# Three MLPs on one Trainium2 core: 2x2 blocks with seven block products in place of eight

## The chip, the core and the metric

The kernel runs on one core of a Trainium2 chip. Five engines work side by side, each through its own queue and in that queue's order: PE (TensorE, matrix products into PSUM), DVE (VectorE), ACT (ScalarE), POOL (GpSimd) and SP (SyncE), which here issues most of the DMAs. The metric is the device time of one execution in microseconds; the median of three runs is quoted.

## What is computed

Three blocks follow each other on 1024 tokens of 1024 features in float32. Each has a mixer (gated delta rule and neighbourhood attention; sliding-window attention and a convolution; gated linear attention) with an output projection, and an MLP of width 4096 with a residual and norms around it. The change is in the MLPs. Cut to the first:

```python
x = layer_norm(DEEPNORM_ALPHA * x + mix, ln1_g[l], ln1_b[l])
ff = jnp.square(jax.nn.relu(jnp.einsum('btd,df->btf', x, w1[l]) + b1[l]))
ff = jnp.einsum('btf,fd->btd', ff, w2[l]) + b2[l]
x = layer_norm(DEEPNORM_ALPHA * x + ff, ln2_g[l], ln2_b[l])
```

The other two have no bias, a residual without factor, and RMS norms; the second norm of the last block gives the output.

## The kernel before

**Exact products.** A float32 operand is kept as a high part (rounded by an ACT cast) and a low part (the rest, a DVE subtraction). `mm3` (L215 to L219) makes a product from three: high by high, high by low, low by high. `unit` (L198) loads up to 1024 elements per partition of a weight matrix into one of two `raw` tiles and splits them into one of `wbufs` = 4 tiles `whi` and `wlo`.

**Order of the work.** The program is written in one sequence; the library places each engine's instructions in a queue when the kernel is built, by priority, and adds the waits. Weights are moved ahead (`high_priority`, `UP` = 6000 instructions); nothing else in the MLPs is ordered by hand. Row tiles pass their norms in stages (`pipe`, `advance`, `flush`): each call takes every row tile under way one stage further.

**PSUM.** Eight banks: two tiles `d` of two banks (`psd`), two tiles `m` and two tiles `s` of one bank each (`psm`, `psp`; `psy` takes them in turn).

**Around an MLP** (`out_mlp`). First come the output projection's products for each row tile of 128 tokens, their addition to the residual X (8 row tiles in SBUF), and the norm, whose last stage `to_xt` (L325) transposes the row tile (8 transposes on PE) and splits it into XT, feature-major, in two halves of 512 tokens (`xt0`, `xt1`). Then `up(f)` makes 128 hidden features for all tokens: 2 token halves x 8 k x 3 products with N = 512, Relu and square on ACT, the square again on POOL and the low part on DVE (L1077 to L1082). `fm_two` makes the first two such blocks, both for the first half of the tokens before the second half, between which the pending row tiles are finished. After five blocks the loop over c (8 steps) takes four hidden blocks, multiplies them with 512 rows of w2 for each token tile t and column half (4 k x 3 products) and adds the result to X on DVE (L1109), and makes the next four hidden blocks. In the last step each row tile of X is complete after its two halves and `done` norms it for the next block or for the output.

**Places.** The two halves of XT, the mixer's output and the hidden tiles live in pools that alternate between the two sides of SBUF. The hidden layer never leaves SBUF.

## Time and profile before

| | us |
|---|---|
| median of three runs | 3921.47 |
| lowest, highest | 3918.44, 3923.11 |
| span of the profiled execution | 3909.3 |
| PE busy | 3723.6 (95%) |
| DVE busy | 1734.8 (44%) |
| ACT busy | 1131.1 (29%) |
| POOL busy | 744.4 (19%) |

The span runs from the first to the last instruction of the program; the profile gives no other time for that execution, so 12.2 us lie between its span and the median. Matmuls overlap on PE, so their durations don't add up: the distance between the starts of two is what one costs. The first MLP runs from about 817 to 1531, the second from about 1982 to 2705, the third ends the kernel.

### The profile page before, as it was taken

What the parts mean: (1) busy time and instruction counts of PE and PEld (TensorE: products, weight loads), DVE (VectorE), ACT (ScalarE), POOL (GpSimd) and SP (SyncE); (2) the same over time, 40 slices, a digit from 0 to 9 for tenths busy, and PEclk for the clock granted to TensorE, in tenths of its full rate; (3) what the DMA queues carried; (4) which work ended last, traced back from release to release, by engine and by line L of the source; (5) the groups of instructions that cost most, each with busy time, mean ns of one, the idle gap of its engine ahead of it and who ended that gap; (6) DMA issues with size and microseconds to landing.
All of it is one profiled execution on the core that took longest, in us unless ns stands there. A gap on an engine that the chain in (4) does not pass through costs nothing.

```text
span 3909.3 us, 46321 instructions
## 1 busy us (share of the span) xinstructions
PE 3723.6 (95%) x19060; PEld 3045.7 (78%) x19060; DVE 1734.8 (44%) x2844; ACT 1131.1 (29%) x1889; POOL 744.4 (19%) x583
## 2 busy tenths in 40 slices
PE   8898898999999999878999999999999999999999
PEld 7777776678888887666778888888788878888887
DVE  7676625552222327896532222224536342222223
ACT  3233334431111123447531111113422231111112
POOL 2011113231200004677310000001112100000001
PEclk9999999999999999988999999999999999999999
DMA  4212235221111112211111111111111211111111
GB/s 158 66 48 57 71 127 172 70 54 49 49 44 44 49 60 98 49 33 33 60 54 44 44 43 43 56 58 43 43 59 49 92 60 49 49 49 44 44 43 70
DMA packets 247160, 237.14 MB, mean 61 GB/s; under 512 B 39467, under 2 KB 208872, under 8 KB 246308
## 3 DMA queue, kind: packets, MB, share of 16 engines
q1 hardware_dynamic: 243492, 227.88, 19.5%
q10 hardware_dynamic: 3456, 6.29, 0.4%
q8 instruction: 150, 2.46, 0.3%
q14 instruction: 62, 0.51, 0.0%
HBM read 197.96 MB, written 36.18 MB: 60 GB/s over the span
## 4 chain that ended last, share of the span: by engine, by line
PE 50%; DVE 5%; issue 2%; POOL 2%; ACT 1%; DMA 0%; POOLq 0%; DVEq 0%; ACTq 0%
PE d L217 8%; PE d L219 8%; PE d L218 8%; PE s L219 4%; PE m L217 4%; PE s L218 4%; PE s L217 4%; PE m L219 4%; PE m L218 4%; PE s L1849 1%; DVE acc L1259 1%; DVE t L1259 1%; POOL st L1253 1%; DVE wlo L206 1%; PE d L1466 1%
## 5 line engine op out<-in xcount | busy, mean ns | idle before, releaser
L206 ACT CAST whi<-raw 128x1024 fp32r<-128x1024 f32 (+1 forms) x283 | 293.8, 1048 | 1751.8 <-PE d L218 657.4
L206 DVE TENSOR_TENSOR wlo<-raw,whi 128x1024 fp32r<-128x1024 f32 (+1 forms) x283 | 355.1, 1263 | 684.6 <-ACT whi L206 684.1
L1081 POOL TENSOR_TENSOR r<-r 128x1024 f32<-128x1024 f32 x96 | 181.8, 1894 | 1778.3 <-ACT hh L1080 1758.0
L217 PE MATMUL d<-xt0h,whi 128*128 128x512 f32 x1152 | 461.2, 400 | 7.1 <-DVE X L1385 5.8
L219 PE MATMUL d<-xt0h,wlo 128*128 128x512 f32 x1152 | 459.7, 399 | 7.6 <-DVE wlo L206 7.6
L218 PE MATMUL d<-xt0l,whi 128*128 128x512 f32 x1152 | 458.9, 398 | 0.0
L217 PE MATMUL d<-xt1h,whi 128*128 128x512 f32 (+1 forms) x1152 | 449.8, 391 | 0.3
L219 PE MATMUL d<-xt1h,wlo 128*128 128x512 f32 (+1 forms) x1152 | 448.9, 390 | 0.0
L218 PE MATMUL d<-xt1l,whi 128*128 128x512 f32 (+1 forms) x1152 | 448.5, 389 | 0.0
L219 PE MATMUL m<-whi,hl 128*128 128x512 f32 x768 | 303.9, 396 | 1.5 <-DVE hl L1082 1.5
L219 PE MATMUL s<-whi,hl 128*128 128x512 f32 x768 | 303.9, 396 | 0.6 <-DVE hl L1082 0.6
L218 PE MATMUL m<-wlo,hh 128*128 128x512 f32 x768 | 303.1, 395 | 0.0
L218 PE MATMUL s<-wlo,hh 128*128 128x512 f32 x768 | 302.5, 394 | 0.0
L217 PE MATMUL m<-whi,hh 128*128 128x512 f32 x768 | 301.2, 392 | 0.1
L217 PE MATMUL s<-whi,hh 128*128 128x512 f32 x768 | 301.3, 392 | 0.0
L219 PEld LDWEIGHTS d<-xt0h,wlo 128*128 128x128 f32 x1152 | 218.5, 190 | 60.8 <-DVE wlo L206 15.9
L217 PEld LDWEIGHTS d<-xt0h,whi 128*128 128x128 f32 x1152 | 218.9, 190 | 54.9 <-issue 8.3
L1109 DVE TENSOR_TENSOR X<-X,m 128x512 f32<-128x512 f32 x184 | 126.2, 686 | 292.2 <-PE m L219 292.0
L218 PEld LDWEIGHTS d<-xt0l,whi 128*128 128x128 f32 x1152 | 218.8, 190 | 45.7 <-issue 0.9
L218 PEld LDWEIGHTS d<-xt1l,whi 128*128 128x128 f32 x1152 | 218.3, 190 | 44.3 <-DVE xt1l L335 1.5
L217 PEld LDWEIGHTS d<-xt1h,whi 128*128 128x128 f32 x1152 | 217.9, 189 | 43.9 <-ACT xt1h L334 1.2
L219 PEld LDWEIGHTS d<-xt1h,wlo 128*128 128x128 f32 x1152 | 218.5, 190 | 42.8 <-issue 0.2
(523 smaller groups left out, 6485.6 us busy)
## 6 DMA issues: line engine op xcount, KB each, us to landing
raw<-in_w_dram SPq DMA_DIRECT2D x64, 512.0 KB
raw<-in_w_in_dram SPq DMA_DIRECT2D x62, 512.0 KB
raw<-in_w_mlp_up_dram SPq DMA_DIRECT2D x32, 512.0 KB
raw<-in_w_mlp_down_dram SPq DMA_DIRECT2D x32, 512.0 KB
raw<-in_w_up_dram SPq DMA_DIRECT2D x32, 512.0 KB
raw<-in_w_down_dram SPq DMA_DIRECT2D x32, 512.0 KB
raw<-in_w_out_dram SPq DMA_DIRECT2D x24, 512.0 KB
X<-xres SPq DMA_DIRECT2D x12, 512.0 KB
```

Source lines behind the costliest of these rows:

```text
L206: self.split = nc.scalar.copy(hi, raw), nc.vector.tensor_tensor(lo, raw, f32v(hi), op=ALU.subtract), ld
L217: mm(out, ah, bh, start=first, stop=False)
L218: mm(out, ah, bl, start=False, stop=False)
L219: mm(out, al, bh, start=False, stop=last)
L1081: nc.gpsimd.tensor_tensor(r, r, r, op=ALU.mult)
L1109: V.tensor_tensor(xs, xs, p, op=ALU.add)
L1253: P.tensor_tensor(ac[:, q : q + 512], ac[:, q : q + 512], tp, op=ALU.add)
L1259: V.scalar_tensor_tensor(out=ac[:, q : q + wd], in0=h[:, q + k : q + k + wd], scalar=cw[:, n, k : k + 1], in1=ac[:, q : q + wd], op0=ALU.m ...
L1466: T.matmul(pd[:, a + 4 * g], PT[:, g, k], vt[:, t + 1 - nk + k, 64 * g : 64 * g + 64], start=k == 0, stop=k == nk - 1)
L1849: T.matmul(ps[g][:, 128 * c : 128 * c + 128], a, x, start=True, stop=True)
```

## The change

Each MLP product is cut into 2x2 blocks, and seven block products (Winograd's form of Strassen's method) take the place of eight. For the up product the blocks are halves of the tokens and halves of the features on one side, and halves of the features and pairs of 128 hidden columns on the other.

- `feed` takes the place of `to_xt` in the norms before an MLP: it keeps the transposed row tile as it is (`a1`, `a2`), splits the blocks that are used alone (L[0], L[1], L[6]) and, from the second half of the tokens on, makes sums on POOL and DVE. `feed_sums` then splits the four sums (L[2] to L[5]).
- The row tiles of X go to DRAM (`spill`) and are added back in the down pass.
- `up_pair` makes 2 x 128 hidden columns for all tokens: `up_weights` loads and combines the weights, seven products of 12 matmuls each go into three banks (`p_`, `r_`, `q_`), ACT and DVE take partial results out while later products add to the same banks, and the four hidden blocks with three of their sums are written to DRAM (`hd`), from one of two places in X.
- After all 16 pairs the down pass runs 4 steps c of 7 products s: for each s the layer's block is loaded from `hd` and split (ACT, POOL), the weights' block is split (ACT, DVE), with sums on POOL at s = 2, and 4 token tiles x 12 matmuls follow. Results are added into quarters of X: s = 5 of the last step completes the first four row tiles, s = 6 the other four.
- The pools of the two XT halves and the mixer's output become fixed places p0 to p3 that stay, with three more (q0 to q2) in the MLPs; block 3's mixer pool changes sides, and block 2 keeps five transposed query tiles instead of six.

The core of the diff (the removed `out_mlp` is printed above):

```diff
+    def mm3(self, out, ah, al, bh, bl, first, last, more=False):
...
+    def slot(self, tag, shape, dt=F32R):
+        pool = self.qp if tag[0] == "q" else self.pa if tag < "p2" else self.pb
+        return self.t(pool, shape, dt, tag=tag)
...
+    def feed(self, t, y):
+        nc = self.nc
+        V, A, T, P = nc.vector, nc.scalar, nc.tensor, nc.gpsimd
+        L = self.L
+        if t == 0:
+            L.update({n: self.slot(f"q{n}", [128, 2, 4, 512]) for n in (0, 1)})
+            L["a1"] = self.slot("q2", [128, 2, 4, 512], F32)
+        if t == 4:
+            L["a2"] = self.slot("p0", [128, 2, 4, 512], F32)
+            L[6] = self.slot("p1", [128, 2, 4, 512])
+        ts = slice(128 * (t % 4), 128 * (t % 4) + 128)
+        raw = L["a1" if t < 4 else "a2"]
+        for q in range(2):
+            p = self.psm().rearrange("p (k c) -> p k c", k=4)
+            for k in range(4):
+                T.transpose(p[:, k], y[:, (4 * q + k) * 128 : (4 * q + k + 1) * 128], self.ident)
+            A.copy(raw[:, q, :, ts], p)
+            if t < 4 or q:
+                o = L[q if t < 4 else 6]
+                A.copy(o[:, 0, :, ts], p)
+                V.tensor_tensor(o[:, 1, :, ts], p, f32v(o[:, 0, :, ts]), op=ALU.subtract)
+        if t >= 4:
+            a1 = L["a1"]
+            s1, s3 = (x[:, :, ts] for x in self.sums())
+            P.tensor_tensor(s1, raw[:, 0, :, ts], raw[:, 1, :, ts], op=ALU.add)
+            V.tensor_tensor(s3, a1[:, 0, :, ts], raw[:, 0, :, ts], op=ALU.subtract)
+            P.tensor_tensor(a1[:, 0, :, ts], s1, a1[:, 0, :, ts], op=ALU.subtract)
+    def sums(self):
+        return [self.X[:, 2 * n : 2 * n + 2].rearrange("p t (k c) -> p (t k) c", k=2) for n in range(2)]
+    def halves(self, o, x):
+        for k in (slice(0, 2), slice(2, 4)):
+            self.nc.scalar.copy(o[:, 0, k], x[:, k])
+            self.nc.vector.tensor_tensor(o[:, 1, k], x[:, k], f32v(o[:, 0, k]), op=ALU.subtract)
+    def feed_sums(self):
+        L = self.L
+        a1 = L["a1"]
+        s1, s3 = self.sums()
+        L[2] = self.slot("p0", [128, 2, 4, 512])
+        self.halves(L[2], a1[:, 0])
+        L[3] = self.slot("p2", [128, 2, 4, 512])
+        self.halves(L[3], s1)
+        L[4] = self.slot("p3", [128, 2, 4, 512])
+        self.halves(L[4], s3)
+        self.nc.vector.tensor_tensor(s1, a1[:, 1], a1[:, 0], op=ALU.subtract)
+        L[5] = self.slot("q2", [128, 2, 4, 512])
+        self.halves(L[5], s1)
+    def parts(self, x, n):
+        nc = self.nc
+        hi, lo = (self.t(self.wp, [128, self.WN], F32R, tag=tag, bufs=self.wbufs)[:, :n] for tag in ("whi", "wlo"))
+        if len(x.shape) == 3:
+            hi, lo = (y.rearrange("p (a b) -> p a b", a=x.shape[1]) for y in (hi, lo))
+        nc.scalar.copy(hi, x)
+        nc.vector.tensor_tensor(lo, x, f32v(hi), op=ALU.subtract)
+        return hi, lo
+    def up_weights(self, w1v, p):
+        nc = self.nc
+        V = nc.vector
+        with self.tc.high_priority(offset=UP):
+            raw = []
+            for q in range(2):
+                r = self.t(self.wp, [128, self.WN], tag="raw", bufs=2).rearrange("p (a b) -> p a b", a=8)
+                nc.sync.dma_start(out=r, in_=w1v[:, :, 256 * p + 128 * q : 256 * p + 128 * q + 128])
+                raw.append(r)
+            b1, b2 = raw
+            u = self.parts(b1, 1024)
+            ta = self.t4().rearrange("p (a b) -> p a b", a=8)
+            V.tensor_tensor(ta[:, 4:], b2[:, :4], b1[:, :4], op=ALU.subtract)
+            V.tensor_tensor(ta[:, :4], b2[:, 4:], ta[:, 4:], op=ALU.subtract)
+            a = self.parts(ta, 1024)
+            tc = self.st().rearrange("p (a b) -> p a b", a=8)
+            V.tensor_tensor(tc[:, :4], b2[:, 4:], b2[:, :4], op=ALU.subtract)
+            V.tensor_tensor(tc[:, 4:], b1[:, 4:], ta[:, :4], op=ALU.subtract)
+            c = self.parts(tc, 1024)
+            b = self.parts(b2[:, 4:], 512)
+        half = lambda x, n: tuple(y[:, 4 * n : 4 * n + 4] for y in x)
+        return half(u, 0), half(u, 1), half(a, 0), half(a, 1), half(c, 0), b, half(c, 1)
+    def up_pair(self, w1v, p, bt, hd):
+        nc = self.nc
+        V, A, P = nc.vector, nc.scalar, nc.gpsimd
+        W = self.up_weights(w1v, p)
+        L = self.L
+        d = self.psd()
+        p_, r_, q_ = d[:, :512], d[:, 512:], self.psy()
+        def prod(n, out):
+            more = n in (2, 4, 5, 6)
+            for k in range(4):
+                self.mm3(out, W[n][0][:, k], W[n][1][:, k], L[n][:, 0, k], L[n][:, 1, k], k == 0 and not more, k == 3, more)
+        Xf = self.X.rearrange("p t d -> p (t d)")
+        o = 4096 * ((p + 1) % 2)
+        hs = Xf[:, o : o + 3584].rearrange("p (n c) -> p n c", n=7)
+        h21 = Xf[:, o + 3584 : o + 4096]
+        b = [bt[:, 2 * p + q : 2 * p + q + 1] if bt is not None else 0.0 for q in range(2)]
+        fn = AF.Copy if bt is None else AF.Identity
+        h11, h12, h22 = hs[:, 0], hs[:, 1], hs[:, 6]
+        def square(h):
+            A.activation(h, h, AF.Relu)
+            P.tensor_tensor(h, h, h, op=ALU.mult)
+        prod(0, p_)
+        A.activation(h11, p_, fn, bias=b[0])
+        prod(1, q_)
+        V.tensor_tensor(h11, h11, q_, op=ALU.add)
+        square(h11)
+        prod(2, p_)
+        A.activation(h12, p_, fn, bias=b[1])
+        prod(3, r_)
+        A.activation(h22, r_, fn, bias=b[1])
+        prod(4, p_)
+        V.tensor_tensor(h22, h22, p_, op=ALU.add)
+        square(h22)
+        prod(5, r_)
+        V.tensor_tensor(h12, h12, r_, op=ALU.add)
+        square(h12)
+        prod(6, p_)
+        A.activation(h21, p_, AF.Relu, bias=b[0])
+        P.tensor_tensor(h21, h21, h21, op=ALU.mult)
+        s1, s2, s3, s4 = (hs[:, n] for n in (3, 2, 4, 5))
+        P.tensor_tensor(s1, h21, h22, op=ALU.add)
+        P.tensor_tensor(s2, s1, h11, op=ALU.subtract)
+        P.tensor_tensor(s3, h11, h21, op=ALU.subtract)
+        P.tensor_tensor(s4, h12, s2, op=ALU.subtract)
+        nc.sync.dma_start(out=hd[:, :, p].rearrange("n p c -> p n c"), in_=hs)
+    def out_mlp(self, w_out, alpha, norm, w1, b1, w2, b2, done, nxt=None):
...
+        V, A, T, P = nc.vector, nc.scalar, nc.tensor, nc.gpsimd
...
+        xr = self.xres.rearrange("(t p) d -> p t d", p=128)
+        self.qp = self.pool("ops", "right")
+        self.L = {}
...
+        self.flush()
+        self.feed_sums()
...
+            bt = self.t(self.tmp, [128, 32], tag="b1")
...
+        if not hasattr(self, "hd"):
+            self.hd = self.dram([7, 128, 16, 512], "hd")
+        hd = self.hd
+        for p in range(16):
+            self.up_pair(w1v, p, bt, hd)
+        half = lambda q, t, c: X[:, 4 * q + t, 512 * c : 512 * c + 512]
+        into = ((0, 0), (0, 0), (0, 1), (1, 1), (1, 1), (0, 1), (1, 0))
+        wtags = (("q0", "q1"), ("q2", "p1")) * 2
+        htags = ["p0", "p2", "p3"] * 7 + ["q0", "p2", "p3"] * 3
+        begun = set()
+        G = {}
+        for c in range(4):
+            w = []
+            with self.tc.high_priority(offset=UP):
+                for g in range(2):
+                    r = self.slot(wtags[c][g], [128, 2, 2, 1024], F32)
+                    for q in range(2):
+                        k0 = 8 * c + 4 * g + 2 * q
+                        nc.sync.dma_start(out=r[:, q], in_=w2v[:, k0 : k0 + 2])
+                    w.append([r[:, :, a, 512 * b : 512 * b + 512] for a in range(2) for b in range(2)])
+            ds = [self.psd() for _ in range(2)]
+            ps = [ds[t // 2][:, 512 * (t % 2) : 512 * (t % 2) + 512] for t in range(4)]
+            rs = [None] * 4
+            t2 = [None] * 2
+            for s in range(7):
+                H = self.slot(htags[7 * c + s], [128, 2, 4, 512])
+                W = []
+                with self.tc.high_priority(offset=UP):
+                    raw = f32v(H[:, 1])
+                    for g in range(2):
+                        gs = slice(2 * g, 2 * g + 2)
+                        nc.sync.dma_start(out=raw[:, gs], in_=hd[s, :, 4 * c + 2 * g : 4 * c + 2 * g + 2])
+                        A.copy(H[:, 0, gs], raw[:, gs])
+                        P.tensor_tensor(H[:, 1, gs], raw[:, gs], f32v(H[:, 0, gs]), op=ALU.subtract)
+                    for g in range(2):
+                        b11, b12, b21, b22 = w[g]
+                        if s == 2:
+                            t2[g] = (self.st if g else self.t4)().rearrange("p (a b) -> p a b", a=2)
+                            P.tensor_tensor(b11, b12, b11, op=ALU.subtract)
+                            P.tensor_tensor(t2[g], b22, b11, op=ALU.subtract)
+                            P.tensor_tensor(b12, b22, b12, op=ALU.subtract)
+                            P.tensor_tensor(b21, b21, t2[g], op=ALU.subtract)
+                        W.append(self.parts((b11, b21, t2[g], b11, b12, b22, b21)[s], 1024))
+                for t in range(4):
+                    ts = slice(128 * t, 128 * t + 128)
+                    if s in (1, 3):
+                        rs[t] = self.psy()
+                    out = rs[t] if s in (1, 3, 5) else ps[t]
...
+                        wh, wl = (x[:, k % 2] for x in W[k // 2])
+                        more = s in (2, 4, 5, 6)
+                        self.mm3(out, H[:, 0, k, ts], H[:, 1, k, ts], wh, wl, k == 0 and not more, k == 3, more)
+                    x = half(into[s][0], t, into[s][1])
+                    if (t, into[s]) in begun:
+                        V.tensor_tensor(x, x, out, op=ALU.add)
...
+                        begun.add((t, into[s]))
+                        A.copy(x, out)
+                    if c == 3 and s >= 5:
+                        if nxt is not None and t == 0:
+                            if s == 5:
+                                self.XT = [self.xt_half(0), None]
+                            else:
+                                self.XT[1] = self.xt_meta() if nxt == "meta" else self.xt_half(1)
+                        done(t + 4 * (s - 5), X[:, t + 4 * (s - 5)])
+                if c in (1, 2) and s >= 3:
+                    for t in (4 * (c - 1) + s - 3,):
+                        r = self.g3()
+                        nc.sync.dma_start(out=r, in_=xr[:, t])
+                        P.tensor_tensor(X[:, t], X[:, t], r, op=ALU.add)
+            if c == 0 and b2 is not None:
+                b2t = self.gbtile(b2, self.g3())
+                for t in range(8):
+                    P.tensor_tensor(X[:, t], X[:, t], b2t, op=ALU.add)
+        self.qp.release()
...
+    def spill(self, t, x, alpha=1.0):
+        if alpha != 1.0:
+            self.nc.scalar.activation(x, x, AF.Copy, scale=alpha)
+        self.nc.sync.dma_start(out=self.xres.rearrange("(t p) d -> p t d", p=128)[:, t], in_=x)
...
-                    qTs[t] = self.t(m, [128, 4, 128], tag="qT", bufs=6)
+                    qTs[t] = self.t(m, [128, 4, 128], tag="qT", bufs=5)
...
+            self.spill(t, x)
+            self.pipe(*self.rms_stages(t, x, G[0], lambda y: self.feed(t, y)))
```

## Rows read from the trace of the kernel before

**Rows 1.** The page's first part: busy us of the span, share, instructions.
```profile
PE 3723.6 (95%) x19060; PEld 3045.7 (78%) x19060; DVE 1734.8 (44%) x2844; ACT 1131.1 (29%) x1889; POOL 744.4 (19%) x583
```

**Rows 2.** Busy time by stretch: us, engines, granted clock, DMA share, GB/s.
```profile
core 0: us, PE busy (x) PEld busy (x) DVE busy (x) ACT busy (x) POOL busy (x), PEclk, DMA share, GB/s
840.00:1490.00 650.00, 650.00 (x2822) 528.20 (x2821) 186.39 (x203) 127.77 (x124) 78.83 (x40) 1.00 0.17 50
1490.00:1534.00 44.00, 42.07 (x195) 32.88 (x194) 39.45 (x64) 16.57 (x24) 28.81 (x18) 1.00 0.22 84
1534.00:1565.00 31.00, 23.48 (x104) 18.00 (x103) 23.98 (x33) 12.77 (x19) 8.66 (x8) 0.89 0.43 136
...
1997.00:2660.00 663.00, 662.57 (x2860) 535.97 (x2859) 188.93 (x206) 127.09 (x126) 60.59 (x32) 1.00 0.16 48
...
3201.00:3860.00 659.00, 658.72 (x2859) 534.81 (x2860) 188.45 (x207) 127.01 (x126) 60.04 (x32) 1.00 0.16 47
```

**Rows 3.** Timeline of PE in the first MLP: start us, us, instruction.
```profile
841.44 0.39 PE L217 MATMUL d<-xt1h,whi 128*128 128x512 f32 x1
...
842.80 0.39 PE L217 MATMUL d<-xt1h,whi 128*128 128x512 f32 x1
```

**Rows 4.** Groups by line and shape, ACT, DVE, POOL: busy us, mean ns.
```profile
L206 ACT CAST whi<-raw 128x1024 fp32r<-128x1024 f32 x278 | 289.2, 1050 | 1749.6 <-PE d L218 657.4 <-PE s L219 551.1 <-PE m L219 302.7
...
L334 ACT CAST xt0h<-m 128x512 fp32r<-128x512 f32 x48 | 27.1, 583 | 74.7 <-PE m L332 74.6
...
L206 DVE TENSOR_TENSOR wlo<-raw,whi 128x1024 fp32r<-128x1024 f32 x278 | 349.5, 1266 | 684.4 <-ACT whi L206 683.9
L1109 DVE TENSOR_TENSOR X<-X,m 128x512 f32<-128x512 f32 x184 | 126.2, 686 | 292.2 <-PE m L219 292.0
...
L1081 POOL TENSOR_TENSOR r<-r 128x1024 f32<-128x1024 f32 x96 | 181.8, 1894 | 1778.3 <-ACT hh L1080 1758.0 <-issue 20.3
```

**Rows 5.** The same view: 512 elements while DVE and POOL both work.
```profile
L1259 DVE SCALAR_TENSOR_TENSOR acc<-X,cw,acc 128x512 f32<-128x512 f32 x30 | 39.1, 1305 | 2.3 <-ACT acc L1388 1.3
...
L1253 POOL TENSOR_TENSOR acc<-acc,tp 128x512 f32<-128x512 f32 x30 | 49.3, 1643 | 42.2 <-issue 20.3 <-ACT tp L1252 19.9
...
L1417 POOL TENSOR_TENSOR xt0l<-X,xt0h 128x512 fp32r<-128x512 f32 x8 | 10.6, 1329 | 1.9 <-ACT xt0h L1416 1.8
```

**Rows 6.** Timeline around the start of an MLP, block 1, then block 2.
```profile
817.01 1.21 DVE L1001 TENSOR_TENSOR X<-X,d 128x1024 f32<-128x1024 f32 x1
...
825.82 2.38 POOL L316 TENSOR_TENSOR X<-X,st 128x1024 f32<-128x1024 f32 x1 [1.26 <-ACT X L310]
...
1981.36 0.40 PE L219 MATMUL s<-whi,xt1l 128*128 128x512 f32 x1
...
1983.36 0.68 DVE L1034 TENSOR_TENSOR X<-X,s 128x512 f32<-128x512 f32 x1
...
1986.88 1.28 DVE L1135 SCALAR_TENSOR_TENSOR t<-X,col,g 128x1024 f32<-128x1024 f32 x1 [0.66 <-POOL col L283]
...
1994.38 1.04 PE L332 MATMUL m<-tri,st 128*128 128x128 f32 x8
1996.38 1.25 PE L332 MATMUL m<-tri,t 128*128 128x128 f32 x8 [0.96 <-DVE xt1l L335]
```

**Rows 7.** Timeline of PE after the first MLP.
```profile
1551.56 0.39 PE L219 MATMUL d<-xt0h,wlo 128*128 128x512 f32 x1
...
1563.38 0.63 PE L217 MATMUL d<-xt1h,whi 128*128 128x512 f32 x1
1563.81 0.63 PE L218 MATMUL d<-xt1l,whi 128*128 128x512 f32 x1
...
1564.97 0.39 PE L218 MATMUL d<-xt1l,whi 128*128 128x512 f32 x1
```

**Rows 8.** Busy time by stretch: two stretches with heavy DMA.
```profile
15.00:21.00 6.00, 5.72 (x35) 5.40 (x35) 5.97 (x10) 2.96 (x5) 3.27 (x2) 1.00 1.02 414
923.00:928.00 5.00, 5.00 (x24) 4.13 (x23) 1.31 (x3) 1.05 (x1) 0.00 (x0) 1.00 0.79 210
```

More of the change, by code (lines that the diff above doesn't have):

```diff
@@ L213, in behind @@
         return ins
-    def mm3(self, out, ah, al, bh, bl, first, last):
+    def mm3(self, out, ah, al, bh, bl, first, last, more=False):
         mm = self.nc.tensor.matmul
-        mm(out, ah, bh, start=first, stop=False)
-        mm(out, ah, bl, start=False, stop=False)
-        mm(out, al, bh, start=False, stop=last)
+        kw = {"skip_group_check": True} if more else {}
+        mm(out, ah, bh, start=first, stop=False, **kw)
+        mm(out, ah, bl, start=False, stop=False, **kw)
+        mm(out, al, bh, start=False, stop=last, **kw)
     def fm(self, w, c0):
@@ L1179, in done @@
             self.pipe(lambda: L.extend(self.ln_stats(x, 1e-5)), scale, square, tx)
-        self.out_mlp(None, "left", "right", "left", ALPHA, norm, i["w1"][0], i["b1"][0], i["w2"][0], row("b2"), done)
+        self.out_mlp(None, ALPHA, norm, i["w1"][0], i["b1"][0], i["w2"][0], row("b2"), done, "xt")
     def b2_mixer(self):
@@ L1577, in b2_mixer, with rms_feed @@
         m.release()
-    def b2_mlp(self):
-        i = self.i
-        row = lambda n: i[n].rearrange("o n -> (o n)")
+    def rms_feed(self, gain):
         G = {}
@@ L2029, in emit @@
     k.b3_mlp()
[L2030 removed]
+    for p in (k.pb, k.pa, k.wp, k.xp, k.ps, k.dr, k.tmp, k.cst):
         p.release()
```

123 lines of the change are left out of this document (30 added, 93 removed).

## The prediction

> **What bounds the kernel now.** I read the busy times first: PE is busy for 95% of the span, DVE for 44%, ACT for 29%, POOL for 19% [rows 1]. A busy PE is not yet a bound, so the second view is the busy time by stretch. In the first MLP (840 to 1490) PE is busy in all of its 650 us at a granted clock of 1.00, that is at 2.4 GHz, while DVE has 186 us, ACT 128 us, POOL 79 us, and the DMA engines a share of 0.17 [rows 2]; the other two MLPs look alike (662.6 of 663 and 658.7 of 659 us). Third, the spacing inside it: a product of an MLP step starts at 841.44 and the sixth after it at 842.80 [rows 3], so one 128x512 product costs 1.36/6 = 0.2267 us, whatever its own duration of 0.39 us says (they overlap). The MLPs are therefore bound by the number of products on PE and by nothing else. Each MLP has 1536 products in its up part (32 column blocks, 2 token halves, 8 k, 3 passes) and 1536 in its down part (8 steps, 8 token tiles, 2 halves, 4 k, 3 passes): 3072 x 0.2267 = 696 us, three times.
>
> **The term removed.** Up: 16 pairs x 7 block products x 4 k x 3 passes = 1344. Down: 4 steps x 7 x 4 token tiles x 4 k x 3 = 1344. That is 2688 for 3072 of the same shape (128 rows, 512 columns), 384 less: 384 x 0.2267 = 87.1 us for each MLP, **261.2 us** in all. It comes off one for one only as long as PE stays the last to finish in each stage, so every other part of the change is held against the new PE time.
>
> **The up pass in steady state.** A pair has 84 products, 19.0 us. ACT: three casts of 1024 (1.05 each) and one of 512 (0.58), four PSUM evictions (0.58), three Relus (about 0.6): 8.0 us [rows 4]. DVE: three low parts of 1024 (1.27) and one of 512 (0.69), four sums of 512 of the weights (0.69), three additions out of PSUM (0.69): 9.3 us [rows 4]. POOL: four squares and four sums of 512. The nearest rows are 1.89 us for 1024 undisturbed, so 0.95 [rows 4], and 1.33 for 512 beside a busy DVE [rows 5]: 7.6 to 10.6 us. None reaches 19.0. DMA: 1.05 MB of weights in and 7 x 128 x 2 KB = 1.84 MB out; the trace shows 210 GB/s for weights in pieces of 512 bytes, with a share of 0.79, and 414 GB/s in large pieces at the start of the kernel [rows 8]: 7 to 14 us of 19.0. The finer test is the reuse of PSUM: products 2, 4, 5 and 6 of a pair write a bank that holds an earlier one, and each has the time of one product in between, 12 x 0.2267 = 2.7 us, for an eviction of 0.6 to 0.7 us to be done. One low part of 1.27 us ahead of it in the queue still fits. The weights of the next pair have a set of four buffers, each freed at least four products (10.9 us) before its successor is used. I take 0.1 us a pair, 5 us in all; ends 0 and 50 (1 us a pair, if two low parts stand ahead).
>
> A rule stands against this. The rows show DVE at 1.31 us for 512 elements out of two SBUF inputs while POOL runs its additions at 1.64 us [rows 5], against 0.69 with one input in PSUM [rows 4]. The Trainium skill says why in "GPSIMD Engine Reference", Specifications: the two engines share SBUF ports, and DVE instructions with two SBUF inputs contend. This case's trace agrees by those numbers. With 1.9 times the price on its eight such operations DVE would need 7.3 x 1.9 + 2.1 = 16 us of a pair, still under 19.0, so the sum stays; the chance of the rivals that lie in waiting is the larger for it.
>
> **The down pass in steady state.** A step s has 48 products, 10.9 us. ACT: two casts of the layer and two of the weights, 4.2 us, and in c = 0 four copies at 0.58. DVE: two low parts and four additions, 5.3 us. POOL: two low parts of 1.89, 3.8 us; at s = 2 eight sums of 1024 more, 15.2 us, which must be done in the 21.8 us of steps 0 and 1 together with the low parts of one or two steps (3.8 each): 19 to 23 us. This is the one place where POOL comes near PE, 12 times. They may start in the step before, so I take 0.3 us each; in block 1 POOL also adds the bias, and in c = 1 and 2 the spilled residual (8 x 1.9 us, beside 76 us of products). Together 4 us; ends 0 and 40.
>
> **The way in.** Before, the first MLP products need only tokens 0 to 511, and 48 of them (10.9 us) hide the norm of the last rows: in block 2 the last projection product starts at 1981.36, its eviction at 1983.36, the scaled row is ready at 1986.88 + 1.28, and the transposes stand at 1994.38 and 1996.38, with a wait of 0.96 us [rows 6]. After, only products 0 and 1 of the first pair (24, 5.4 us) work on the first half alone; product 2 needs sums of all four blocks. From the same row being ready, 6.8 us after the last projection product: transposes 1.0, two raw copies 1.2, two POOL sums 2.6, a cast and a low part 2.3: about 14 us, in which PE has 5.4 us and two sets of transposes (2.1). Then DVE is the last to finish: eight low parts of the sums (10.2), a difference of 2048 elements (2.5), the weights' parts and sums of the first pair (6.0), and 2.8 of smaller things, 21.5 us from 8.9 us on, so product 5 starts at about 30.4 and the pair ends at 35.9, against 21 us of PE work: 15 us lost, 13 more than before. In block 1 the row goes through POOL (until 828.2, 11.2 us after the eviction at 817.01 [rows 6]), and I take 14. **In all 40 us**; ends 24 (the next pair's products 0 and 1 fill in) and 75.
>
> **From up to down.** 4.2 MB of w2 go into places that products 0 and 1 of the last pair free, and the layer's first block (1.05 MB) behind them; the store of the pair before (1.84 MB) is in the same queue. At 414 GB/s that is 17 us, plus a cast and a POOL low part (2.9), against the 16.3 us of six products: 3.7 us lost; at 210 GB/s 20 us. I take 6, since pieces of 2 to 8 KB are nearer to the faster row: **18 us** for three; ends 0 and 60. If the first load waits for the last pair's store, it is 17 each: inside these ends.
>
> **The way out.** DVE is busy for 63 of the 75 us from 1490 to 1565 [rows 2]: the norms of block 1's result are its work, at 6 us a row tile. Row tiles used to be finished every 5.4 us; now they all fall into the last 22 us, 2.7 us apart, so that work starts 19 us later and has 8 evictions less: **10 us** lost there (0 to 20). Blocks 2 and 3 need some 3.5 us of DVE a tile: 3 us for both.
>
> **Clock.** After 1551.56 PE did little but transposes for 10 us, and the products that follow stand 0.43 us apart (1563.38, 1563.81), against 0.2267: the 1.2 GHz level [rows 7]. Up to the one at 1564.97 there are eight of them, 8 x 0.2 = 1.6 us; two or three of the new seams would see it: 4 us.
>
> **Sum:** 261 - 5 - 4 - 40 - 18 - 13 - 4 = 177 us off. The profiled execution spans 3909.3 us, so 3732; the median of the runs is 12.2 us above that span, and I keep this difference: **3744 us**. A smaller measured change than 0.2% (8 us) can't be told from none.
>
> **Rivals.** (a) The seams are filled by later products: 24 for the way in, nothing from up to down, 5 out, 5 for the rest: 227 us off, 3695. For: PE's order is free of such waits everywhere in the MLPs now. Against: DVE's 21 us in the way in have no cover. (b) The four guarded products of a pair wait 0.5 us each on average behind DVE or ACT: 192 x 0.5 = 96 us, 3840. For: the shared work of DVE and POOL [rows 5]; DVE's load in an MLP grows from 29% to about half. Against: 2.7 us of slack. (c) The other side, the same place: at 0.93 us of waiting on each of the 192 the gain is eaten; with one contended low part (1.27 x 1.9 = 2.4) and an addition (1.3) always ahead, less the slack, it is about 1.4 us, 269 us: 4013, slower. (d) The stores bound the up pass: its blocks lie 4 MiB apart in DRAM; if they moved at half of the 210 GB/s, a pair would take 17.5 + 5.0 = 22.5 us for 19.0: 48 x 3.5 = 168 us, 3912. Against: the weights' pieces, 2 MiB apart, already move at 210 with 0.79 of the engines [rows 8]. The Trainium skill has such a rule ("DMA: Bandwidth & Descriptors", Latency and other measured facts: a row pitch of 4 MiB gave 103 GB/s against 207 at 512 KiB); by it the estimate is that of (d). No run here shows that pitch yet.
>
> **Chances.** Forecast (3695 to 3795) 0.58; (a) 0.10; (b) 0.20; (d) 0.04; (c) 0.08. The range leaves out (c), most of (d) and the ends of (a) and (b): 3680 to 3860. Faster 0.90, within 0.2% 0.02, slower 0.08.
>
> **What the profile will show.** Right: products 0.227 us apart at clock 1.00 in both passes, an up pass of about 305 + 15 us and a down pass of about 305 + 6, PE idle only at the seams, and there first behind the low parts on DVE. Wrong, if PE waits inside pairs for ACT or DVE evictions ((b), (c)), for DMA ((d)), or for POOL around s = 2; or if the mixers, whose pools move, come out longer.

## The result and the profile after

After the change the kernel takes 4082.2 us (median of 4 runs, 4078.2 to 4095.4) against 3921.4 before: 1.042 times as long, with an interval of 1.040 to 1.044. The forecast was 3744. The profiled execution spans 4078.0 us, 168.7 more than that of before.

The page's first part, and busy time by stretch in the first MLP: its up pass, the change to the down pass, the down pass (columns as in [rows 2]).

```profile
PE 3603.2 (88%) x17908; PEld 2889.8 (71%) x17908; DVE 2240.2 (55%) x3183; ACT 1527.6 (37%) x2485; POOL 1913.6 (47%) x1183
```

```profile
866.00:1205.00 339.00, 308.73 (x1226) 235.46 (x1226) 179.07 (x162) 116.65 (x164) 177.25 (x120) 0.95 0.42 133
1205.00:1260.00 55.00, 30.16 (x112) 23.16 (x112) 12.58 (x9) 15.97 (x18) 50.58 (x24) 0.78 0.60 225
1260.00:1535.00 275.00, 243.64 (x998) 192.95 (x998) 123.05 (x112) 92.92 (x96) 201.07 (x78) 0.95 0.36 127
```

PE fell from 95% to 88% [rows 1], and where it was busy in all of an MLP at a granted clock of 1.00 [rows 2] it now idles in each stage, at 0.78 to 0.95. POOL went from 19% to 47%. No other engine is full over the span, so this is in the main a matter of waits, not of work; only between the passes is POOL busy for 50.6 of 55 us.

**Inside the up pass** the store of a pair comes every 23.0 us (mean of 13 intervals in each MLP: 22.83, 23.03, 23.07), not 19.04. Once a pair PE stops. The waits of PE in one pair, and ACT, DVE and POOL around it (start us, us, instruction, idle before and what ended it):

```profile
PE d L219 <- ACT X L1163: 1.8, 1, 1.8
```

```profile
1045.63 1.04 ACT L1101 CAST whi<-t 128x1024 fp32r<-128x1024 f32 x1 [4.82 <-DVE t L1119]
1046.58 0.68 ACT L1163 ACTIVATE X<-d,b 128x512 f32<-128x512 f32 x1
1041.54 0.83 DVE L1118 TENSOR_TENSOR t<-raw,raw 128x512 f32<-128x512 f32 x1 [2.12 <-DMA raw<-in_w_dram]
1042.30 1.77 DVE L1122 TENSOR_TENSOR st<-raw 128x512 f32<-128x512 f32 x1
1044.00 1.52 DVE L1119 TENSOR_TENSOR t<-raw,t 128x512 f32<-128x512 f32 x1
1041.79 1.73 POOL L1175 TENSOR_TENSOR X<-X 128x512 f32<-128x512 f32 x1
1043.48 1.49 POOL L1153 TENSOR_TENSOR X<-X 128x512 f32<-128x512 f32 x1
```

Read it backwards. PE stands 1.80 us for the eviction of h22 (L1163). ACT stood still for 4.82 us at the instruction ahead of it, a cast (L1101) of the *next* pair's third weights, which waited for DVE's sums (L1119), which waited for a weight load and then ran at 1.5 to 1.8 us beside POOL, against 0.69 where they ran alone. These weights are used some 15 us later. After the stop eight products follow at 0.37 to 0.43 us, the 1.2 GHz level, which costs 1.5 us more; so it is in 28 of the 39 pairs counted, while the stops of the other 11 are followed by none. In all a pair has 3.2 us over the 19.8 of the first experiment. Over the whole kernel, the groups of instructions (busy us, mean ns, idle before and its ends):

```profile
L219 PE MATMUL d<-p,whi 128*128 128x512 f32 x1072 | 460.2, 430 | 103.4 <-ACT X L1163 80.9 <-ACT p L1077 9.6 <-DVE X L1567 6.5
L1101 ACT CAST whi<-t 128x1024 fp32r<-128x1024 f32 x60 | 62.8, 1046 | 321.6 <-DVE t L1119 210.2 <-PE d L221 54.1 <-issue 34.4
L219 PE MATMUL d<-whi,p 128*128 128x512 f32 x864 | 363.6, 423 | 119.4 <-DVE X L1269 66.6 <-ACT X L1272 50.0 <-ACT p L984 1.9
L1247 POOL TENSOR_TENSOR p<-p 128x1024 fp32r<-128x1024 f32 x150 | 394.0, 2645 | 202.3 <-ACT p L1246 202.2
L1102 DVE TENSOR_TENSOR wlo<-q,whi 128x1024 fp32r<-128x1024 f32 x108 | 188.4, 1745 | 233.0 <-ACT whi L1101 228.7 <-DMA q<-in_w_dram 1.8 <-DMA q<-in_w_down_dram 1.8
```

The last three are the down pass: POOL's low part takes 2.65 us where the forecast had 1.89 [rows 4], DVE's 1.75 where it takes 1.27 alone, and PE waits 66.6 us for DVE's additions out of PSUM and 50.0 for ACT's copies (the latter all in the stops between the passes, below). In one place an addition stands behind a low part of weights that runs beside a sum of POOL, and PE waits 2.0 us for it:

```profile
1325.43 3.41 DVE L1102 TENSOR_TENSOR wlo<-p,whi 128x1024 fp32r<-128x1024 f32 x1
1328.77 0.68 DVE L1269 TENSOR_TENSOR X<-X,d 128x512 f32<-128x512 f32 x1
```

**Between the passes** PE's waits, then POOL and SP (pair 15's chain is L1153 to L1177, its store L1178):

```profile
PE d L219 <- ACT X L1272: 16.0, 1, 16.0
PE d L221 <- POOL p L1247: 7.5, 1, 7.5
```

```profile
1237.50 2.42 POOL L1256 TENSOR_TENSOR q<-q,st 128x1024 f32<-128x1024 f32 x1
1239.88 2.40 POOL L1247 TENSOR_TENSOR p<-p 128x1024 fp32r<-128x1024 f32 x1
1242.23 2.02 POOL L1153 TENSOR_TENSOR X<-X 128x512 f32<-128x512 f32 x1
...
1250.10 1.26 POOL L1177 TENSOR_TENSOR X<-X 128x512 f32<-128x512 f32 x1
...
1225.89 0.88 SPq L1232 DMA_DIRECT2D p<-in_w_dram  x2
1226.87 0.41 SPq L1178 DMA_DIRECT2D hd<-X  x1
1242.31 0.82 SPq L1245 DMA_DIRECT2D p<-hd  x2
1251.38 0.37 SPq L1178 DMA_DIRECT2D hd<-X  x1
```

The down pass's low parts and weight sums, which have priority, stand ahead of pair 15's squares and sums on POOL, so its store is issued at 1251.38. The first eviction of the down pass (L1272) writes the half of X that this store reads; PE waits 16.0 us for it.

**Where the time went.** From PE's rows of each trace I added, for all three MLPs, the idle time before the instructions ("idle") and, for products 0.36 to 0.6 us apart, what is beyond 0.227 ("slow"). The way in runs from 27 us before the last transposes of the norm to 4 us behind the first store, the up pass to 8 us behind the 14th store, the start of the down pass 70 us from there, the down pass to some 5 us before the MLP's end. "MLPs" is from those transposes to the first behind the MLP (in the third to PE's last instruction).

| kernel | way in idle / slow | up pass | start of down | down pass | MLPs us |
|---|---|---|---|---|---|
| before (same places) | 6 / 1 | 0 / 0 | 0 / 0 | 2 / 0 | 2051 |
| after | 44 / 11 | 73 / 45 | 80 / 14 | 83 / 22 | 2237 |
| up_cast_behind | 46 / 9 | 1 / 3 | 77 / 15 | 82 / 23 | 2108 |
| up_no_sums_o | 39 / 8 | 26 / 0 | 37 / 7 | 82 / 25 | 2088 |
| seam_lo_dve | 45 / 11 | 72 / 44 | 61 / 15 | 81 / 17 | 2212 |
| down_lo_dve | 45 / 12 | 74 / 43 | 58 / 18 | 69 / 11 | 2193 |
| down_sums_dve | 44 / 12 | 73 / 45 | 50 / 10 | 121 / 21 | 2235 |
| all_dve_but_res | 46 / 10 | 1 / 4 | 46 / 12 | 65 / 18 | 2047 |
| all_dve | 46 / 11 | 2 / 4 | 49 / 7 | 46 / 12 | 2018 |
| all_dve_c1 | 46 / 11 | 2 / 1 | 52 / 8 | 44 / 15 | 2021 |
| spread | 46 / 11 | 2 / 2 | 45 / 9 | 13 / 5 | 1976 |
| spread_h21 | 46 / 11 | 2 / 2 | 44 / 7 | 14 / 3 | 1973 |
| sums15_dve | 46 / 11 | 3 / 3 | 46 / 7 | 14 / 6 | 1980 |
| feed_dve | 44 / 9 | 1 / 2 | 46 / 7 | 13 / 6 | 1976 |
| store_first | 46 / 13 | 3 / 2 | 46 / 7 | 13 / 7 | 1980 |
| store_first_c1 | 45 / 12 | 2 / 4 | 23 / 6 | 12 / 3 | 1951 |

The time of a single execution can be off by 12 to 16 us for a reason outside the MLPs (last section). The experiments, one execution each where no range is given, are therefore read by this table as well as by their times.

### The profile page after: what moved, and what is told of

Same layout as the page of the kernel before. It is cut to its first block, busy times and chain, and to the rows that moved or that the text cites. A ratio compares the mean times of both kernels' runs of the same rounds, so it can differ in the third digit from the quotient of the medians.

```text
span 4078.0 us, 46523 instructions
## 1 busy us (share of the span) xinstructions
PE 3603.2 (88%) x17908; PEld 2889.8 (71%) x17908; DVE 2240.2 (55%) x3183; ACT 1527.6 (37%) x2485; POOL 1913.6 (47%) x1183
## 4 chain that ended last, share of the span: by engine, by line
PE 56%; DVE 16%; DMA 9%; POOL 8%; issue 6%; ACT 6%; SPq 0%; POOLq 0%; ACTq 0%; DVEq 0%
PE d L219 12%; PE d L220 11%; PE d L221 10%; DVE wlo L1102 3%; ACT whi L1101 2%; PE m L219 2%; PE s L219 2%; PE m L221 2%; PE s L221 2%; PE s L220 2%; PE m L220 2%; DVE st L1122 2%; DVE t L1119 2%; DMA raw<-in_w_mlp_up_dram 1%; DMA raw<-in_w_dram 1%
## 5 line engine op out<-in xcount | busy, mean ns | idle before, releaser
L219 PE MATMUL d<-p,whi 128*128 128x512 f32 (+1 forms) x1152 | 483.5, 420 | 103.4 <-ACT X L1163 80.9
L219 PE MATMUL d<-whi,p 128*128 128x512 f32 (+1 forms) x1056 | 426.9, 406 | 125.9 <-DVE X L1269 66.6
L1247 POOL TENSOR_TENSOR p<-p 128x1024 fp32r<-128x1024 f32 x150 | 394.0, 2645 | 202.3 <-ACT p L1246 202.2
L221 PE MATMUL d<-p,wlo 128*128 128x512 f32 (+1 forms) x1152 | 464.6, 403 | 6.0 <-DVE wlo L206 4.7
L220 PE MATMUL d<-p,whi 128*128 128x512 f32 (+1 forms) x1152 | 465.7, 404 | 4.0 <-DVE p L1078 3.0
L221 PE MATMUL d<-whi,p 128*128 128x512 f32 (+1 forms) x1056 | 409.7, 389 | 27.2 <-POOL p L1247 25.3
L220 PE MATMUL d<-wlo,p 128*128 128x512 f32 (+1 forms) x1056 | 411.2, 389 | 8.2 <-DVE wlo L206 8.2
L1153 POOL TENSOR_TENSOR X<-X 128x512 f32<-128x512 f32 x144 | 194.8, 1354 | 465.5 <-ACT X L1152 465.5
L219 PEld LDWEIGHTS d<-p,whi 128*128 128x128 f32 x1152 | 228.6, 199 | 197.1 <-ACT X L1163 101.4
L219 PEld LDWEIGHTS d<-whi,p 128*128 128x128 f32 x1056 | 213.8, 202 | 207.2 <-DVE X L1269 91.0
L1102 DVE TENSOR_TENSOR wlo<-q,whi 128x1024 fp32r<-128x1024 f32 x108 | 188.4, 1745 | 233.0 <-ACT whi L1101 228.7
L221 PEld LDWEIGHTS d<-p,wlo 128*128 128x128 f32 x1152 | 229.7, 199 | 56.4 <-DVE wlo L206 5.3
L220 PEld LDWEIGHTS d<-p,whi 128*128 128x128 f32 x1152 | 229.4, 199 | 49.2 <-DVE p L1078 4.5
L221 PEld LDWEIGHTS d<-whi,p 128*128 128x128 f32 x1056 | 213.2, 202 | 68.4 <-POOL p L1247 27.0
L220 PEld LDWEIGHTS d<-wlo,p 128*128 128x128 f32 x1056 | 214.0, 203 | 41.1 <-DVE wlo L206 9.0
L1101 ACT CAST whi<-q 128x1024 fp32r<-128x1024 f32 x108 | 113.6, 1052 | 301.5 <-PE d L221 212.0
L1101 ACT CAST whi<-t 128x1024 fp32r<-128x1024 f32 x60 | 62.8, 1046 | 321.6 <-DVE t L1119 210.2
```

The source lines that it names most:

```text
L219: mm(out, ah, bh, start=first, stop=False, **kw)
L220: mm(out, ah, bl, start=False, stop=False, **kw)
L221: mm(out, al, bh, start=False, stop=last, **kw)
L1101: nc.scalar.copy(hi, x)
L1102: nc.vector.tensor_tensor(lo, x, f32v(hi), op=ALU.subtract)
L1153: P.tensor_tensor(h, h, h, op=ALU.mult)
```

## Experiments

The theory: the products were saved as forecast, and queues in a poor order give the time back. Rivals: the seven stores of a pair bound the up pass; DVE and POOL slow each other wherever things stand.

**The order on ACT.** `L["h22"]` is the eviction at L1163 of the pair before.

```diff
+        cast = nc.scalar.copy(hi, x)
+        if prev is not None:
+            self.behind(cast, prev)
...
-            a = self.parts(ta, 1024)
+            a = self.parts(ta, 1024, L.get("h22"))
...
+        L["h22"] = A.activation(h22, r_, fn, bias=b[1])
```

> One thing is changed in the kernel after: on ACT the cast of the third weight sum (b22-b21+b11, used two products into the next pair) stands behind the eviction of h22 instead of ahead of it. Theory A (an order on ACT: this cast waits for a late weight load and for sums of weights on DVE, and the eviction that PE needs waits behind it): the pair's period falls from 23.4 us to 19.2 to 20.0, the granted clock of the up pass comes back to 1.00, 48 pairs give back 160 to 200 us, so 3880 to 3920 us. Rival B (the seven stores of a pair bound it, 1.84 MB a pair): the period stays at 23 or more and the time within 20 us of 4080. Rival C (POOL and DVE slow each other, wherever the cast stands): the wait moves to another product, the period stays above 21.5 and the time above 3990.

3951.9 us, 130 less than after. A row of this kernel's up pass by stretch, and ACT in one pair:

```profile
890.00:1150.00 260.00, 260.00 (x1092) 201.64 (x1090) 164.68 (x143) 103.73 (x143) 153.57 (x103) 0.99 0.47 145
```

```profile
1006.08 0.69 ACT L1165 ACTIVATE X<-d,b 128x512 f32<-128x512 f32 x1 [3.10 <-PE d L221]
1007.35 1.05 ACT L1101 CAST whi<-t 128x1024 fp32r<-128x1024 f32 x1 [0.58 <-DVE t L1121]
```

The eviction (now L1165) goes first, PE is busy in all of the 260 us, the store comes every 20.0, 19.7 and 19.7 us. The same 1.84 MB a pair are stored, so the stores bound nothing at this pace. The gain is under the expected 160: that took 23.4 us for each of 48 pairs, where the mean was 23.0, and 3.2 us in the 39 intervals counted are 125. A pair keeps 0.75 us more than 84 x 0.2267.

The sums of H (`s1` to `s4` on POOL) left out, the cast kept ahead of the eviction:

> The four sums of H on POOL are left out (four of the seven arrays stored hold old data), and the cast is held ahead of the eviction of h22 on ACT, as in the kernel after. Theory A with the sums of the weights slowed by POOL (1.77, 1.52 and 0.83 us where 0.69 is the price alone): they end 2.0 us earlier, the eviction follows 2.0 us earlier, PE's wait of 1.8 us goes, the period is 19.2 to 20.5 and the time 3870 to 3950. Theory A with the late load alone as the cause: the wait shrinks by less than 1 us and the period stays above 21.5, the time above 3990. Rival B (stores): as after, 23 us and 4060 to 4080, since the stores are unchanged.

3939.8 us. Only part of the wait goes: 26 us idle are left in the up pass of 73, in stops of 0.6 to 1.2 us, and none of them is followed by slow products. So POOL's sums beside DVE were part of the lateness; the rest may be the late weight load, which no run took away. The order alone, without touching either, removes the wait.

**POOL in the down pass.** For the first two products only, then for all, the low part of H on DVE (`P.tensor_tensor(H[:, 1, gs], ...)` becomes `V.tensor_tensor`):

> The low part of H goes to DVE for the first two products of the down pass alone. Theory F (the down pass's low parts on POOL keep pair 15's squares and sums, and so its stores, waiting; the first eviction of the down pass writes the buffer of that store): the 16 us wait for the eviction falls below 8 and the 7.5 us wait for the low part to 2, 10 to 18 us for each MLP, 4025 to 4050. Rival G (the stores wait in the queue of SP behind loads that wait for their slots): the 16 us stay, at most 5 us each from the first wait, 4062 to 4078.

> In the whole down pass the low part of H is made on DVE (1.22 us) instead of POOL (2.4 to 3.4 us). Theory D (POOL is late in the down pass and at its start: it has 14 low parts, 8 weight sums and residual or bias sums a step of 76 us, and pair 15's squares and sums stand behind its low parts): the gaps of 2 to 5 us inside the down pass go, and part of the 16 us at its start, 20 to 40 us for each MLP, so 3960 to 4020. Rival E (DVE has 27 us more in each step and its additions out of PSUM come late): the waits stay with DVE's addition named, within 15 us of 4078 or slower.

4053.2 and 4041.1 us. The start of the down pass has 61 and 58 us idle instead of 80; the 16 us wait became 14.5 and 11.0, so the first theory overstated it: weight sums on POOL still stand ahead of pair 15. In the second the down pass has 14 us less idle. The other half alone, L1253 to L1256 on DVE:

> The kernel after with one edit: the eight sums of down weights of a step are on DVE (about 1.25 us each, beside nothing) instead of POOL (2.4 to 3.4). Theory D (POOL is overfull in the down pass, and what it does beside DVE makes both slower: a low part on DVE takes 3.2 to 3.4 us beside a POOL sum, 1.22 alone): at the start pair 15's squares and sums no longer stand behind 24 us of weight sums, the 16 us wait falls below 8, and the gaps after each third product of a step shrink: 10 to 22 us for each MLP, 4012 to 4048. Rival E (DVE becomes late instead): within 15 us of 4078.

4076.9 us, no gain, as rival E had it. Groups of this kernel:

```profile
L219 PE MATMUL d<-whi,p 128*128 128x512 f32 x864 | 358.6, 418 | 124.7 <-DVE X L1269 91.9 <-ACT X L1272 29.9 <-ACT p L984 1.9
L1254 DVE TENSOR_TENSOR st<-q 128x1024 f32<-128x1024 f32 x6 | 20.3, 3387 | 0.0
```

The start has 30 us less idle, the pass 38 more: on DVE beside POOL's low parts six such sums take 3.39 us on the mean, and the additions that PE needs stand behind them (66.6 became 91.9). Both halves on DVE, on top of the order on ACT, then the residual and bias sums too:

> The kernel with the cast moved behind the eviction of h22 (3950 us), and in the down pass the low parts of H and the sums of weights on DVE; POOL keeps only the residual and bias sums there. Theory D: DVE has about 60 us of work in 76 us of a step and nothing beside it, the start of the down pass waits under 8 us for the store of pair 15, the down pass under 8 us in all: 20 to 30 us for each MLP, 3860 to 3890. Rival E (DVE in order is too full, its additions out of PSUM come late): 3920 or more.

> As the run before it, and the residual and bias sums on DVE as well (1.25 us each instead of 2.4), so POOL has nothing in the down pass after pair 15's sums. If what is left of the gaps came from POOL's slow bias sums (which hold the buffer that the residual's load needs, and that load stands ahead of the loads of H on SP) or from sums on both engines at once, it is 4 to 8 us faster in the MLP that has the bias and 2 to 4 us in each other: 8 to 16 us under the run before it. If DVE is full, it is slower than that.

3901.0 and 3856.3 us (16 of the 45 between them lie outside the MLPs; the 29 inside are more than the 8 to 16 expected, while the first misses its 3860 to 3890). With POOL out of the down pass the same instructions take (groups of the second):

```profile
L1249 DVE TENSOR_TENSOR p<-p 128x1024 fp32r<-128x1024 f32 x150 | 183.6, 1236 | 61.4 <-ACT p L1248 60.5
L1104 DVE TENSOR_TENSOR wlo<-q,whi 128x1024 fp32r<-128x1024 f32 x108 | 133.6, 1237 | 119.7 <-ACT whi L1101 118.2
```

against 2645 on POOL and 1745 on DVE in after: one engine does it sooner than two that share.

**What stands behind what on DVE.** In that kernel PE still stopped for 7.0 to 9.3 us twice a MLP. DVE before one such stop:

```profile
1335.91 2.35 DVE L1255 TENSOR_TENSOR q<-q 128x1024 f32<-128x1024 f32 x2
1338.18 1.22 DVE L1256 TENSOR_TENSOR t<-q 128x1024 f32<-128x1024 f32 x1
1339.32 1.22 DVE L1257 TENSOR_TENSOR q<-q 128x1024 f32<-128x1024 f32 x1
1340.45 1.22 DVE L1249 TENSOR_TENSOR p<-p 128x1024 fp32r<-128x1024 f32 x1
1341.59 1.22 DVE L1256 TENSOR_TENSOR st<-q 128x1024 f32<-128x1024 f32 x1
1342.73 1.22 DVE L1249 TENSOR_TENSOR p<-p 128x1024 fp32r<-128x1024 f32 x1
1343.86 1.22 DVE L1257 TENSOR_TENSOR q<-q 128x1024 f32<-128x1024 f32 x1
1345.00 1.27 DVE L1271 TENSOR_TENSOR X<-X,d 128x512 f32<-128x512 f32 x2
```

Nine microseconds of sums and low parts with priority stand ahead of the two additions (L1271). The sums were put into the loop over token tiles of s = 1, without priority:

```diff
-                        if s == 2:
...
+                    if s == 1:
+                        g, sub = t % 2, ALU.subtract
...
+                        if t < 2:
...
+                            V.tensor_tensor(b11, b12, b11, op=sub)
+                            V.tensor_tensor(t2[g], b22, b11, op=sub)
+                        else:
+                            V.tensor_tensor(b12, b22, b12, op=sub)
+                            V.tensor_tensor(b21, b21, t2[g], op=sub)
```

> The kernel with all of the down pass on DVE (3854.6 us in its profile), and the eight sums of down weights no longer made in one go for the third product: two of them after each token tile's addition of the second product, at the place in the program, without priority. Theory H (the two waits of 7.4 to 9.7 us a MLP for an addition out of PSUM, at the third product of steps two and three, are an addition that stands behind 10 us of sums and low parts on DVE; at the start of the pass the same sums hold pair 15's addition): both go, with 1 to 3 us each for the clock after them, and 3 to 5 us at the start of the pass: 17 to 28 us for each MLP, 3775 to 3805. Rival (the sums are then late for the third product's weights): as long or longer, 3845 or more.

3826.7 us, with 12 more outside the MLPs than all_dve. The down pass fell from 46 to 13 us idle and the MLPs by 42 us; 51 or more were expected, since nothing went at the start of the pass. Stops of 2.7 us are left where there were 7.0.

**The store of pair 15.** What is left is the start of the down pass: 13.0, 10.4 and 11.4 us idle in one stop, for the copy that waits for this store. Four edits, each on top of the last: the Relu of h21 ahead of the step's third casts on ACT; pair 15's square and sums on DVE; the loads of H behind the stores on SP and two weight sums behind pair 15's on DVE; last, the loads of the second step's down weights behind the store.

```diff
+        E = V if p == 15 else P
...
+        E.tensor_tensor(h21, h21, h21, op=ALU.mult)
...
+                        if c == 0 and s in (2, 3):
+                            self.behind(ld, self.L["st" if s == 3 else "prev"])
...
+                        if c == 1:
+                            self.behind(ld, self.L["st"])
```

> As the run before it, and on ACT the casts of the first step's third weights stand behind the Relu of pair 15's h21, which they made wait in the run with all on DVE. The store of pair 15 is what the first eviction of the down pass waits for; if ACT's order holds it, the wait at the start of the pass falls by 2 to 5 us for each MLP, 6 to 15 us under the run before it; if the chain of POOL's four sums (6 us) and the store (6 us) alone are left, within 4 us of it.

> As the run with spread sums and the Relu first (3807 us), and for pair 15 alone the square of h21 and the four sums are on DVE (0.69 us each, 3.4 us) instead of POOL (1.7 to 2.3 us each beside DVE, 10.5 us). PE waits 10 to 13.5 us at the start of the down pass for the eviction that waits for this pair's store. If the chain of sums holds the store, the wait falls by 5 to 8 us for each MLP and the time by 15 to 27 us; if the store waits for its turn in the DMA queues behind 4 MB of down weights and 1 MB of H, by less than 2 us each.

> As the run with pair 15's sums on DVE (PE waits 14.0, 11.5 and 11.5 us at the start of the down passes), with the order of the queues set: on SP the loads of H for the third and fourth product of the first step stand behind the stores of pairs 14 and 15 (there the store of pair 15 had its sums at 1201.1 and was issued at 1203.97, behind a load that waits for its slot), and on DVE the last two weight sums of the first step stand behind pair 15's sums. Theory K (the queues' order holds the store): issued 4 to 6 us earlier, the wait falls to 6 to 9 us, 12 to 20 us in all. Theory L (the DMA engines: 4 MB of the second step's weights are issued just ahead of the store and 410 GB/s need 10 us for them): issued earlier, landed as before, the wait stays above 10 us.

> As the run before it, and the second step's 4 MB of down weights stand behind the store of pair 15 on SP. Theory K: within 5 us of the run before it. Theory L: the wait falls to 0 to 4 us and the time by 20 to 35 us against the run with pair 15's sums on DVE. With both: 3770 to 3795 us.

3808.3, 3833.4, 3818.1, and 3794.8 us (4 runs, 3787.6 to 3805.1). The first three leave 44 to 46 us idle there. The fourth halves it: 4.9, 6.2 and 3.1 us in that stop. Queues of SP in the third and the fourth, and the copy that waits:

```profile
1187.77 0.79 SPq L1249 DMA_DIRECT2D p<-hd  x2
1188.62 0.43 SPq L1236 DMA_DIRECT2D p<-in_w_dram  x1
1189.14 0.41 SPq L1182 DMA_DIRECT2D hd<-X  x1
1201.01 1.07 ACT L1271 COPY X<-d 128x512 f32<-128x512 f32 x2 [7.46 <-DMA hd<-X]
```

```profile
1187.53 0.37 SPq L1182 DMA_DIRECT2D hd<-X  x1
1194.83 1.08 ACT L1273 COPY X<-d 128x512 f32<-128x512 f32 x2 [3.22 <-DMA hd<-X]
```

Issued at about the same time, the store is through 11.9 us later behind 1 MB of the second step's weights and 1 MB of H that were issued just ahead of it, and 7.3 us later without them (in the fourth this load of H, too, comes behind the store): DMA time. The same move alone, on the kernel all_dve, had done nothing:

> As the run before it, and the loads of the second step's down weights (4 MB, 10 us at the 405 GB/s of the start of the down pass) are queued on SP behind the store of pair 15. If the wait for that store at the start of the down pass is one for DMA time, it falls by 4 to 10 us for each MLP, 12 to 30 us under the run before it; if POOL's sums alone held it, it is within 5 us of that run.

3873.7 us (14 of the difference to all_dve outside the MLPs), 52 us idle there. In all_dve the store was issued late, at 1197.4, and the copy ran 6.2 us later: the weights were through by then, and there was nothing to be ahead of. So this edit was worth nothing while the store was issued late. Which of the edits between all_dve and the fourth one it needs was not run one by one.

**The way in.** The two POOL sums of each token tile on DVE, on top of sums15_dve:

> As the run before it, and on the way into the MLP the two sums of the tokens that POOL makes for each token tile (1.3 to 2.2 us each beside DVE) are on DVE (0.69). If these sums keep POOL's part of the next token's norm and its bias addition waiting, and PE's transposes behind them (a wait of 8 us before the last transposes of the first MLP, 9 us in the third), 5 to 9 us go in the first MLP and 2 to 6 in each other, clock and all 9 to 20 us. If DVE is then late for the halves that the third product needs, within 5 us of the run before it.

3819.4 us (4 runs, 3812.4 to 3825.2; 0.976 of before, 0.975 to 0.978), 44 us idle for 46: this theory fell. What PE waits for there is in the next section; no run moved it.

**Against before**, store_first_c1 takes 0.970 of its time (0.968 to 0.972): 3794.8 for 3912.0 on the same chip.

## Why the prediction was wrong

**The term removed held.** In the stretches of "MLPs" lie 8857 products before and 7944 in the others (the rest of the 1152 fall outside their ends): 913 x 0.2267 = 207 us less. Against before, after has there 265 us more idle, 90 more slow and 39 of wider spacing; that is 187 us longer, and 186 were measured. store_first_c1 has 66, 23 and 17; that is 101 us shorter, and 100 were measured. The 0.2267 itself is that of an undisturbed six: over the first MLP before the mean is 650 / 2822 = 0.2303 [rows 2].

**Up pass: 5 forecast, about 154 measured** (73 idle, 45 slow, 36 for 0.75 us a pair of spacing, the difference of 19.8 and 19.04). The step that failed is "one low part of 1.27 us ahead of it in the queue still fits". I priced what might stand ahead of a guarded eviction by its duration; the cast ahead took 1.04 us, and waited 4.8. That the next pair's weights find free buffers early, which I gave as a reason for no wait, lets their cast, which has priority, stand in front. No busy time shows this: ACT has 37%. The place was that of rivals (b) and (c), but one of the four guarded products waits and not all four; the 118 us of idle and slow are nearer to the 96 of (b) than to the 269 of (c). That the time came out nearest to (c) (4013 us, chance 0.08) is luck of the sum, for two other stages add the rest; and (c)'s 1.4 us a wait doesn't follow from its terms (2.4 + 1.3 less 2.7 is 1.0). Rival (d) is refuted by up_cast_behind. In the half microseconds in which the packets of a store moved alone there, they moved at 201 to 385 GB/s. The Trainium skill's rule on pitches ("DMA: Bandwidth & Descriptors", Latency and other measured facts) is for rows. Here rows lie 32 KiB apart and only the seven blocks 4 MiB, so I applied it where it doesn't hold, and no run here shows it.

**From up to down: 18 forecast, 94 measured** (80 and 14). I summed bytes of loads against six products. The first load of H did not wait for the last store (issued at 1200.17, the store at 1251.38). What was missing is that the first *eviction* must wait for it, since it writes the buffer that the store reads, and that work with priority passes pair 15's on POOL and SP: the moved step's own queues were not walked through.

**Down pass: 4 forecast, 105 measured** (83 and 22). The place was named, POOL around s = 2; the price was wrong. POOL's 1.89 us [rows 4] are those of a square of one tile with itself; with two different inputs it takes 2.38 us alone, as L316 in [rows 6] already did, and 2.65 on the mean of the low parts. And I did not charge DVE for it. The rule from "GPSIMD Engine Reference", Specifications (the Trainium skill), that DVE contends with POOL where both its inputs are in SBUF, was weighed for the up pass only, on busy time. The trace of after bears it out for both engines (128x1024: DVE 1.22 us alone, up to 3.5 beside POOL; POOL 2.38 alone, 3.38 beside DVE). As bounds of "0 and 40" came from work sums, neither end knew of an addition that waits behind a low part of 3.41 us.

**Way in: 40 forecast, 38 idle and 10 slow measured.** The size came out right, the place did not, so this is largely luck. DVE's low parts of the sums (L1078), which were to finish last and to cost 13 us or more in each MLP, hold PE for 3.2 us in all three. Waits of PE in after in the first, the second and the third MLP:

```profile
PE m L1057 <- POOL X L318: 7.4, 1, 7.4
PE d L220 <- DVE p L1078: 2.0, 1, 2.0
PE d L219 <- ACT p L1077: 8.4, 1, 8.4
```

Of the 44 us idle 18 lie ahead of the last transposes (7.4 for POOL's addition in the norm, the rest in the main for low parts out of PSUM), 9.6 wait for ACT's casts of the sums, 8.3 for evictions of the first pair, 4.1 for casts of weights.

**Way out: 13 forecast**, about 12 measured. In the 80 us from the first transposes behind the MLP idle and slow together are 22 against 10 in block 1, and 3 against 4 in block 2. The largest wait there is for DVE's part of the norm (10.8 us), as forecast.

**Clock: 4 forecast, 91 measured** (the slow columns, already in the stages above). The mechanism was in [rows 7]; I counted two or three seams, but in the up pass it follows 28 of 39 stops. A stop in the up pass cost 1.6 times its length (73 and 45).

These sum to 154 + 94 + 105 + 48 + 12 = 413, so 152 us slower than before by the 261; measured were 169 in the profiled executions. Of the other 17 us some 9 lie at the end of the first mixer (the second is 2 us longer, the third 4 shorter). There this wait was 3.2 us before, and the granted clock from 750 to 790 is 0.70 where it was 0.91:

```profile
PE m L891 <- DVE o L883: 7.5, 2, 5.8
```

Its cause was not followed up, and some 10 us stay open. The 12.2 us that I kept between span and time are no constant either: in each execution with both on record the time is 1.6 to 1.9 us above the span.

## What to carry to other kernels

Before an engine's order is called free of waits, write down for each instruction that stands ahead of a PSUM eviction what *it* waits for, not how long it takes; work that is prefetched early is the first suspect. When a product count falls, the queues of the stages between (a store that an eviction must wait for, loads with priority ahead of that store) become the path, and moving a load out of the way pays only once the store itself is issued early. Before splitting elementwise work with two SBUF inputs between DVE and POOL near the path, price it beside the other engine and not alone: here all of it on DVE was faster.

## What the runs showed of the hardware

Of the 39 stops of PE in the up pass of after (1.5 to 3.0 us, most of them 1.80 or 1.81), 28 were followed within a dozen products by six to twelve at the 1.2 GHz level (up to 0.43 us apart), 11 of 1.5 to 1.8 us by none; so their length alone does not decide it. In up_no_sums_o, in the same stage, stops of 0.64 to 1.18 us were followed by none.

DVE and POOL slowed each other on operations with both inputs in SBUF: with 128x1024 a low part on DVE took 1.22 us alone and up to 3.5 beside POOL, one on POOL 2.38 alone and 3.38 where DVE worked beside it all the time. DVE's additions with one input in PSUM (128x512) took 0.63 to 0.69 us in every kernel, though in after 154 of the 288 ran wholly beside POOL.

One stretch ahead of the MLPs, whose code no edit touches, came at a granted clock of 0.95 in some executions and 0.80 or 0.81 in others, with nearly the same busy time; in these what follows comes 12 to 16 us later. First spread, then spread_h21:

```profile
400.00:500.00 100.00, 88.70 (x549) 72.91 (x550) 56.02 (x185) 33.07 (x82) 13.96 (x16) 0.81 0.20 60
```

```profile
400.00:500.00 100.00, 88.81 (x703) 72.35 (x704) 57.48 (x188) 35.04 (x89) 14.98 (x19) 0.95 0.28 82
```

In the first PE has 549 recorded products where the second has 703. A time from a single execution is no better than this.
